# First gate weights split beside the input projection, half of layer 1's adaLN beside layer 0's attention, V projected amid head 0's K and Q

## The chip, the cores and the metric

The kernel runs on one core of one Trainium2 chip. The metric is the device time of one execution in microseconds, from 3 runs; a profile is one further execution. TensorE (PE; PEld is its weight load) multiplies matrices, VectorE (DVE) and ScalarE (ACT) work element by element and can read PSUM, GpSimd (POOL) works on SBUF, SyncE (SP) issues DMAs.

## The reference

Two layers of a diffusion backbone work on 1024 latent tokens and 256 context tokens of width 1024. Each layer modulates its input with adaLN, mixes tokens, gates the result with a SiLU branch, projects it, and normalises the sum with the residual:

```python
shift, scale, gate = adaln(c, ada_w[i], ada_b[i])        # silu(c) @ w + b, split in 3
shift_c, scale_c, gate_c = adaln(c_ctx, ada_w[i], ada_b[i])
h = x * (1.0 + scale[:, None, :]) + shift[:, None, :]
h_c = ctx * (1.0 + scale_c) + shift_c
...                                                      # token mixer i, gated
x = layer_norm(DEEPNORM_ALPHA * x + gate[:, None, :] * (o @ out_w[i]), ln_g[i], ln_b[i])
if need_ctx:
    ctx = layer_norm(DEEPNORM_ALPHA * ctx + gate_c * (o_c @ out_w[i]), ln_g[i], ln_b[i])
```

Layer 0 is multi-head latent attention with 16 heads: one projection of h gives a 256-wide Q latent, a 128-wide KV latent, 32 rotary key columns and the 1024 gate columns; the latents are RMS-normalised and projected up to Q, K (64 + 32 wide) and V (64 wide). Latent tokens attend to latent and context tokens, context tokens to the context. Layer 1 is differential attention with 8 heads.

## The kernel before, in words

Products of float32 operands are made of three matmuls (`mm3`, lines 185 to 188): each operand is split into a high part on ScalarE and a low remainder on VectorE or GpSimd (`split`, lines 176 to 178). Code that is not inside a `manual_schedule` block is reordered on each engine by a scheduler with a cost model, which takes the program order as preference; inside such a block the engines named (`MAN = 'P'`: TensorE alone) keep the written order. Pools of SBUF buffers are stacked from two sides; a tile waits until those that held its place have been read.

*Start (lines 204 to 238).* The shift and scale of layer 0 come from 16 loads of adaLN weights. Then h is made in three chunks, the context (256 tokens) and two of 512 latent tokens, in 8 parts each: load, high part on ScalarE, value on VectorE, remainder on VectorE, or on GpSimd for every third part.

*Input projection (lines 266 to 300).* Ten tiles of 128 tokens (context first), each 24 matmuls of 416 columns into PSUM tag "a" or "b" (two banks each). Squares on ScalarE, an inverse root on GpSimd (`rstd_of`) and a scaling on VectorE give the normalised rows `ln`; `lat_post` of the tile before follows: transposes through "c", split into `latH`, `latL`.

*Gates (lines 426 to 448).* The 1024 gate columns go in four quarters. For each, 8 rows of blocks of w_in are loaded and split (`wgs`, `wgH`, `wgL`), then 10 token tiles follow of 24 matmuls each, Silu on ScalarE, and a store to `sg_d` issued by SyncE. After each tile two steps of a generator `beside_gates` run. It holds, first, `up_weights` (lines 302 to 380): the split of the up-projections, the column norms of three weights (squares on ScalarE, a matmul with ones, a maximum on VectorE), the rotated key columns `kr`, and the power-of-two scales `vsc0`, `ksc0`, `qsc0`. Second, `ada_dve` (lines 383 to 419): layer 0's gate rows and all of layer 1's adaLN. Eight chunks (layer, pc) of 512 columns; each loads 8 blocks `adw` of 128 x 512 and adds them, times a column of silu(c), into `acc0` (latent) and `acc1` (context; not for the last two chunks) on VectorE. Matmuls with ones sum over the partitions. At the end `cols1` and `ab1` are made.

*Head 0 (lines 451 to 515, 708 to 715).* A new pool takes the place of h. V's weights are loaded and split in buffers "p32", which lie early in the pool. `prod_k` makes K of two heads at a time, `prod_q` Q with its rotary part; both store rows in a staging tile and copy them by DMA (`dmv`) to where the head needs them. `max0` computes row maxima of the scores on VectorE. `prod_v0` makes V, ten tiles, each in one pair of PSUM banks ("a", three pairs), evacuated by ScalarE and VectorE. In program order K and the first Q come first, then V's tiles with the rest of Q and the maxima between them.

*Attention (lines 605 to 735).* Each head has 11 units: 3 matmuls per 512 scores and key block, exponential and a float16 copy on ScalarE, a remainder on GpSimd (line 609), and the products with V two units later. Beside them run the next head's K, Q and maxima, as counts per unit (`run_step`), TensorE in written order. Head 15 also loads and splits the output weights (`load_outw`, lines 696 to 702).

After that come layer 0's output projection (lines 745 to 818) and layer 1 (from line 821), which the change does not touch.

## Time and profile before

| | us |
|---|---|
| median of 3 runs | 1950.05 |
| lowest, highest | 1944.06, 1951.67 |
| profiled execution | 1947.66 |
| its span, first to last instruction | 1945.9 |
| PE, DVE, ACT, POOL busy | 1749.7, 1283.0, 1033.5, 893.8 |
| mean granted clock of TensorE | 0.962 |

The rows quoted below are of this one execution; times in them count from the start of its span. A row of the timeline gives start, duration, engine, line, operation, output <- inputs, and in brackets the idle time before it with what ended it. A row of a group gives count, busy time, mean in ns, and the idle time before. A row of a window gives its length, the busy time and instructions of each engine (PE, PEld, DVE, ACT, POOL), the granted clock, the busy share of the DMA engines and GB/s.

### The profile page before, as it was taken

Reading aid. Unit: us, or ns where it says so; the run is one execution under the profiler, and the core shown is the slowest. Engines: PE = TensorE matmul, PEld = TensorE weight load, DVE = VectorE, ACT = ScalarE, POOL = GpSimd, SP = SyncE. Lnnn points to the kernel's source line nnn. Section 1 sums busy time; section 2 is a strip of 40 time slices with the busy share of each in tenths; the row PEclk is TensorE's granted clock in tenths of the full one; section 3 lists DMA queues with packets and bytes.
Section 4 is the critical chain, followed back from the end, with each engine's and each line's share of the span. In section 5 each row is a group of like instructions: output and inputs, shape, how many; then the busy total and the mean of one; then the engine's idle time right before and its main releaser. Section 6 shows DMA issues by size and latency. Waiting matters only on the chain. (4 is left out here: it accounts for less than half of the span.)

```text
span 1945.9 us, 36855 instructions
## 1 busy us (share of the span) xinstructions
PE 1749.7 (90%) x14460; PEld 1342.0 (69%) x14460; DVE 1283.0 (66%) x2213; ACT 1033.5 (53%) x2094; POOL 893.8 (46%) x750
## 2 busy tenths in 40 slices
PE   8889969999999998878879998989999999995997
PEld 2778945666666664556658787868787878783666
DVE  2536766666565658337753869686878787878785
ACT  2532127777777777701114565656666666665331
POOL 2433015767767676746663425242424242416322
PEclk9989979999999999989989999999999999997999
DMA  7426650111111113053233111111112121205331
GB/s 252 126 83 195 195 158 22 44 30 36 40 42 33 33 43 105 15 195 116 101 111 90 53 47 50 49 50 46 52 44 57 34 64 37 58 18 194 105 110 62
DMA packets 116366, 155.41 MB, mean 80 GB/s; under 512 B 14448, under 2 KB 85712, under 8 KB 116192
## 3 DMA queue, kind: packets, MB, share of 16 engines
q1 hardware_dynamic: 116192, 153.05, 25.8%
q8 instruction: 114, 1.87, 0.4%
q14 instruction: 60, 0.49, 0.1%
HBM read 99.18 MB, written 27.08 MB: 65 GB/s over the span
## 5 line engine op out<-in xcount | busy, mean ns | idle before, releaser
L609 POOL TENSOR_TENSOR pl<-p,ph 128x1024 f16<-128x1024 f32 (+1 forms) x176 | 362.7, 2066 | 185.7 <-ACT ph L608 160.7
L1046 ACT ACTIVATE p<-ps_b,mx 128x512 f32<-128x512 f32 (+1 forms) x384 | 232.8, 626 | 47.1 <-DVE mx L1043 46.6
L589 DVE TENSOR_REDUCE mx<-ps_a 128x1 f32<-128x1024 f32 x128 | 155.6, 1222 | 135.4 <-PE ps_a L587 135.4
L607 ACT ACTIVATE p<-ps_a,esc 128x1024 f32<-128x1024 f32 (+1 forms) x176 | 189.1, 1074 | 95.1 <-PE ps_a L665 88.4
L183 DVE SCALAR_TENSOR_TENSOR pl<-ps_b,lcf,ph 128x512 f16<-128x512 f32 (+1 forms) x192 | 123.3, 657 | 109.9 <-ACT ph L182 108.4
L608 ACT CAST ph<-p 128x1024 f16<-128x1024 f32 (+1 forms) x176 | 177.0, 1006 | 5.4
L1040 DVE TENSOR_REDUCE mx<-ps_b 128x1 f32<-128x512 f32 x256 | 166.0, 678 | 0.7 <-PE ps_b L1024 0.2
L186 PE MATMUL ps_b<-h1H,wH 128*128 128x512 f32 (+1 forms) x384 | 149.6, 390 | 18.7 <-ACT p L1046 15.7
L186 PE MATMUL ps_b<-wH,h1H 128*128 128x256 f32 x512 | 156.0, 305 | 0.0
L678 PE MATMUL ps_d<-Vh,pl 128*128 128x65 f16 x1344 | 147.6, 195 | 6.3 <-POOL pl L609 6.3
L675 PE MATMUL ps_d<-Vh,ph 128*128 128x65 f16 x1344 | 149.6, 196 | 0.0
L677 PE MATMUL ps_d<-Vl,ph 128*128 128x64 f16 x1344 | 148.3, 194 | 0.0
L187 PE MATMUL ps_b<-wL,h1H 128*128 128x256 f32 x512 | 146.7, 286 | 0.0
L188 PE MATMUL ps_b<-wH,h1L 128*128 128x256 f32 x512 | 146.5, 286 | 0.0
L182 ACT ACTIVATE ph<-ps_b,lcf 128x512 f16<-128x512 f32 (+1 forms) x192 | 120.5, 641 | 42.3 <-PE ps_b L1059 42.3
L188 PE MATMUL ps_b<-h1H,wL 128*128 128x512 f32 (+1 forms) x384 | 138.3, 360 | 4.2 <-POOL wL L178 4.2
L178 POOL TENSOR_TENSOR wL<-ws,wH 128x512 fp32r<-128x512 f32 x64 | 90.9, 1422 | 106.3 <-PE ps_b L187 59.0
L187 PE MATMUL ps_b<-h1L,wH 128*128 128x512 f32 (+1 forms) x384 | 137.7, 359 | 0.0
L675 PEld LDWEIGHTS <-ph 128*128 128x128 f16 x1344 | 124.2, 98 | 18.0 <-issue 5.0
L677 PEld LDWEIGHTS <-ph 128*128 128x128 f16 x1344 | 125.0, 99 | 12.4 <-issue 0.8
L1023 PE MATMUL ps_b<-KS,QS 128*128 128x512 f16 (+1 forms) x384 | 129.7, 355 | 3.8 <-ACT p L1046 2.7
L1024 PE MATMUL ps_b<-KS,Q 128*128 128x512 f16 (+1 forms) x384 | 132.3, 353 | 0.0
(338 smaller groups left out, 5389.4 us busy)
## 6 DMA issues: line engine op xcount, KB each, us to landing
adw<-in_ada_w SPq DMA_DIRECT2D x64, 256.0 KB
ws<-in_dw SPq DMA_DIRECT2D x64, 256.0 KB
g<-sg_d SPq DMA_DIRECT2D x18, 512.0 KB
adaw<-in_ada_w SPq DMA_DIRECT2D x16, 512.0 KB
sg_d<-gg SPq DMA_DIRECT2D x40, 128.0 KB
o<-o_d SPq DMA_DIRECT2D x10, 512.0 KB
o_d<-op SPq DMA_DIRECT2D x7, 640.0 KB
xt<-in_xT SPq DMA_DIRECT2D x16, 256.0 KB
```

The costliest lines, as they stand in the source:

```text
L186: pe.matmul(ps, aH, bH, start=start, stop=False, skip_group_check=skip)
L187: pe.matmul(ps, aH, bL, start=False, stop=False, skip_group_check=skip)
L188: pe.matmul(ps, aL, bH, start=False, stop=stop, skip_group_check=skip)
L589: dve.tensor_reduce(mx[:, t, 0:1], ps, axis=AX.X, op=ALU.max)
L607: act.activation(p32[:, :n], st, AF.Exp, scale=esc0)
L608: act.copy(ph[:, :n], p32[:, :n])
L609: pool.tensor_tensor(pl[:, :n], p32[:, :n], ph[:, :n], op=ALU.subtract)
L675: pe.matmul(pv[:, t, :], ph[:, ts], Vh[:, k, h, :], start=(k == kcs[0] and t == 0), stop=False, skip_group_check=True)
L677: pe.matmul(pv[:, t, :V0], ph[:, ts], Vl[:, k, h, :], start=False, stop=False, skip_group_check=True)
L678: pe.matmul(pv[:, t, :], pl[:, ts], Vh[:, k, h, :], start=False, stop=(k == NT - 1), skip_group_check=True)
L1040: dve.tensor_reduce(mx[:, 2 + 2 * m + i:3 + 2 * m + i], b, axis=AX.X, op=ALU.max, negate=True)
L1046: act.activation(p[m][:, c0:c0 + n], b, AF.Exp, bias=nb, scale=sc1, accum_out=sm[:, 2 + 3 * m + i:3 + 3 * m + i])
```

## The change

TensorE's written order (`man`) now holds from the input projection to the end of V.

1. The splitting of one part of h becomes `h_part`. The context and the first 512 latent tokens are split as before; the last 512 two parts at a time after each of the first four tiles of the projection, with three load buffers.
2. The first quarter's gate weights are loaded and split in the projection's loop, one block per tile; two of the quarter's tiles stand among the last two `lat_post`. The weights of a quarter are split during the quarter before, in two sets of buffers in two pools. The stores of the gates are issued by ScalarE.
3. `lat_post` follows its tile by two instead of one, and the normalisation has high priority.
4. In `up_weights` the rotated keys come ahead of the column norms, a norm's matmuls come a step after its squares, and V's weight for the norm is loaded by ScalarE.
5. `ada_dve` takes its buffers, banks and chunks as arguments; a chunk is closed at the eighth step of the next one. Four chunks remain beside the gates, (0, 4), (0, 5), (1, 0), (1, 1); (1, 2), (1, 3), (1, 4), (1, 5) run as a side of the attention, three steps per head, with two `adw` buffers and sums in the PSUM pairs. `ab1` is made after the attention.
6. "p32" moves to the end of the pool; V's weights use a third "p32" buffer for staging. `prod_v0` steps a whole tile, and starts after head 0's Q projection.

```diff
-    for i, (c0, n) in enumerate((CHUNKS[2], CHUNKS[0], CHUNKS[1])):
+    def h_part(pool_, bufs, c0, n, k):
         s = 0 if c0 < SEQ else 1
...
+    for i in (2, 0):
         for k in range(KT):
+            h_part(hs, 8, *CHUNKS[i], k)
...
+    pgr = p0.enter_context(spool("p0gr", side="right"))
+    def gate_w(pool_, q):
+        wH = pool_.tile([P, KT, 256], F32R, tag="wgH", bufs=1, name=nm("wgH"))
+        wL = pool_.tile([P, KT, 256], F32R, tag="wgL", bufs=1, name=nm("wgL"))
+        yield wH, wL
+        for k in range(KT):
+            ws = pgr.tile([P, 256], F32, tag="wgs", bufs=4, name=nm("wgs"))
+            sp.dma_start(ws, w_in[k * P:(k + 1) * P, NA + q * 256:NA + (q + 1) * 256])
+            split(wH[:, k, :], wL[:, k, :], ws, e_lo=pool)
+            yield
+    gcount = [0, 0, 0, 0]
+    def gate_tile(q, wH, wL):
+        t = gcount[q]
+        gcount[q] += 1
+        ts = slice(t * P, (t + 1) * P)
+        ps = bank("a" if t % 2 == 0 else "d")[:, :256]
+        for k in range(KT):
+            mm3(ps, hH[:, k, ts], hL[:, k, ts], wH[:, k, :], wL[:, k, :], k == 0, k == KT - 1)
+        g = pgr.tile([P, 256], F32, tag="gg", bufs=2, name=nm("gg"))
+        act.activation(g, ps, AF.Silu)
+        act.dma_start(sg_d[0][ts, q * 256:(q + 1) * 256], g)
+    gw = gate_w(pgr, 0)
+    wg = next(gw)
+    man = ExitStack()
+    man.enter_context(tc.manual_schedule(engines={ENG[c] for c in MAN}))
...
+        hk = iter(range(KT))
+        todo = []
+        for t in (8, 9, 0, 1, 2, 3, 4, 5, 6, 7, None, None):
+            if len(todo) == 2 or t is None:
+                lat_post(*todo.pop(0))
+                next(gw, None)
+            if t is None:
+                for _ in gw:
+                    pass
+                gate_tile(0, *wg)
+                continue
...
+            with tc.high_priority():
...
+            todo.append((t, ln))
+            for k in (next(hk, None), next(hk, None)):
+                if k is not None:
+                    h_part(pa, 3, *CHUNKS[1], k)
...
+                for j, f in enumerate(parts):
+                    f(wsq[:, j, :], slice(c0, c0 + 512))
+                yield
+                bk = bank("c")
+                for j, f in enumerate(parts):
+                    pe.matmul(bk, onr, wsq[:, j, :], start=j == 0, stop=j == len(parts) - 1)
...
+            act.dma_start(wv, w_kv[:, 1024 + c.start:1024 + c.stop])
...
+    def ada_dve(tile_, bk_, chunks):
+        def close(layer, pc, acc):
+            if pc < 4:
+                cb = bk_()
+                ns = len(acc)
+                for s in range(ns):
+                    for j in range(4):
+                        pe.matmul(cb[:, 2 * j + s:2 * j + s + 1], acc[s][:, j * P:(j + 1) * P], ones[:, 0:1],
+                                  start=True, stop=True)
...
+        for layer, pc in chunks:
+            acc = [tile_(f"acc{s}") for s in range(1 if layer and pc > 3 else 2)]
             for k in range(KT):
+                w = tile_("adw")
                 sp.dma_start(w, ada_w[layer, k * P:(k + 1) * P, pc * 512:(pc + 1) * 512])
...
+                if k == 7 and done:
+                    close(*done)
                 yield
+            done = layer, pc, acc
+        for _ in range(4):
             yield
+        close(*done)
+        yield
...
+            yield from ada_dve(t_, lambda: bank("c"), ((0, 4), (0, 5), (1, 0), (1, 1)))
...
+            for _ in gw:
+                pass
+            wH, wL = wg
+            if q < 3:
+                gw = gate_w((pg, pgr)[q % 2], q + 1)
+                wg = next(gw)
+            while gcount[q] < NT:
+                gate_tile(q, wH, wL)
+                if gcount[q] > 1:
+                    next(gw, None)
+                for _ in range(2 if q == 1 or q > 1 and gcount[q] % 5 < 3 else 1):
                     next(side, None)
...
+            "ows": ([P, D], F32, 2), "adw": ([P, 512], F32, 2), "acc0": ([P, 512], F32, 1),
+            "acc1": ([P, 512], F32, 1)}
...
     KL[0] = wk.tile([100, NTOK], F16, name="KL0")
+    TAG0["p32"] = [P, 1024], F32, PB[0]
+    rot(wk, *TAG0["p32"][:2], "p32", PB[0], first=True)
...
-    for _ in chain(prod_k(0), prod_q(0, 0)):
-        pass
-    vg, sg = prod_v0(), chain(max0(0, 0), prod_q(0, 1), prod_q(0, 2))
-    for i, _ in enumerate(vg):
-        if i % 2:
-            next(sg, None)
-    for _ in sg:
-        pass
+    vg = prod_v0()
+    if True:
+        for i, _ in enumerate(chain(prod_k(0), prod_q(0, 0), prod_q(0, 1), prod_q(0, 2), max0(0, 0))):
+            if i > 3:
+                next(vg, None)
+        for _ in vg:
+            pass
+    man.close()
+    ada = ada_dve(w0, pair, ((1, 2), (1, 3), (1, 4), (1, 5)))
...
+            run_step(units0(h, 0), [(ada, (0, 0, 1)), (max0(h, 1), (1, 1, 2, 1, 1)), (max0(h, 2), (0, 1, 0, 1)),
                                     (kq, (2, 2, 1 + quad, 0, 0) if even else (2,))])
...
+            run_step(units0(h, 1) + units0(h, 2), [(ada, (0, 0, 1, 0, 1)), (max0(h + 1, 0), (1, 1, 1, 2, 1)),
                                                    (qs, (1, 1 + quad, 0, 1) if even else (2,))])
     flush()
+    assert next(ada, 7) == 7
+    ab1_of()
```

163 lines of the change are left out of this document (63 added, 100 removed).

## The prediction

> **What bounds the kernel now.** I read the page first: TensorE is busy for most of the span, so time can be had where it stands idle.
>
> ```profile
> span 1945.9 us, 36855 instructions
> ...
> PE 1749.7 (90%) x14460; PEld 1342.0 (69%) x14460; DVE 1283.0 (66%) x2213; ACT 1033.5 (53%) x2094; POOL 893.8 (46%) x750
> ...
> PE   8889969999999998878879998989999999995997
> ```
>
> The low digits of the first 300 us are where the change works. I cut that stretch by stage with the windows view: span of the window, then busy time and instructions of PE, PEld, DVE, ACT, POOL, the granted clock, DMA.
>
> ```profile
> 42.25:62.20 19.95, 19.45 (x96) 17.42 (x96) 19.77 (x38) 15.75 (x26) 6.43 (x5) 1.00 0.72 229
> 62.20:67.04 4.84, 0.15 (x1) 0.00 (x0) 4.84 (x10) 1.66 (x8) 3.19 (x5) 0.75 0.21 65
> 67.04:107.50 40.46, 35.51 (x184) 32.42 (x184) 16.89 (x40) 18.30 (x66) 18.48 (x23) 0.92 0.21 61
> 107.50:119.20 11.70, 8.25 (x18) 4.72 (x19) 7.24 (x17) 6.79 (x14) 2.48 (x5) 0.50 0.22 59
> 119.20:252.05 132.85, 128.73 (x1028) 124.18 (x1027) 80.73 (x139) 25.98 (x68) 31.02 (x32) 0.99 0.60 180
> 252.05:264.30 12.25, 2.97 (x6) 0.17 (x5) 6.52 (x10) 0.38 (x1) 1.66 (x2) 0.65 0.57 172
> 264.30:304.90 40.60, 30.12 (x120) 20.62 (x119) 29.56 (x30) 15.75 (x18) 3.99 (x4) 0.85 0.36 105
> 312.00:745.00 433.00, 412.86 (x4917) 265.26 (x4917) 265.44 (x358) 332.42 (x331) 306.70 (x150) 1.00 0.14 36
> ```
>
> These are, in order: the input projection up to its fourth tile; a stop; the other six tiles; the column norms before the gates; the gate projection; the wait for layer 1's adaLN; head 0's K, Q and V up to the first score; and, past a short start, heads 0 to 14 of the attention. In the second row VectorE is full (4.84 of 4.84) while TensorE has one instruction; in the fourth the clock is 0.50 and TensorE does 18 instructions; in the sixth it does 6. In the last row TensorE is busy 95% with VectorE at 61%: there TensorE is the limit. The timeline of TensorE names what ended the stops (start, duration, idle before):
>
> ```profile
> 67.04 0.90 PE L271 MATMUL ps_c<-idr,ln 128*128 128x128 f32 x3 [4.69 <-DVE ln L293]
> ...
> 262.50 1.86 PE L405 MATMUL ps_b<-acc,ones 128*1 128x512 f32 x2 [9.18 <-DVE acc L396]
> 264.30 0.80 PE L186 MATMUL ps_a<-latH,wkH 128*128 128x512 f32 x1
> ...
> 282.69 1.03 PE L587 MATMUL ps_a<-KH,qH 96*128 96x512 f16 x2 [7.51 <-DMA qH<-stpH]
> ```
>
> So the front loses time to late VectorE work: normalised rows behind the splitting of h, the adaLN sums behind the loads of their own weights, and head 0's Q behind rope and a copy.
>
> **The change part by part.** *Input projection.* The lag between a tile's projection and its transposes grows from one tile to two, the normalisation gets priority over the splitting of h, the last 512 tokens of h are split between tiles, and TensorE keeps the written order. The price of a tile when nothing waits is the distance from one set of transposes to the next:
>
> ```profile
> 75.00 0.49 PE L271 MATMUL ps_c<-idr,ln 128*128 128x128 f32 x3
> ...
> 75.35 0.43 PE L186 MATMUL ps_b<-wAH,hH 128*128 128x416 f32 x1
> ...
> 79.98 0.49 PE L271 MATMUL ps_c<-idr,ln 128*128 128x128 f32 x3
> ```
>
> 4.98 us, ten tiles 49.8; from 42.25 that is 92. I add 5: the first four tiles are paced by h (19.95 us without a transpose, where 4 x (79.98 - 75.35) is 18.5), and the last parts of h may be late. VectorE's share of h is this:
>
> ```profile
> L235 DVE TENSOR_SCALAR xt<-xt,cols 128x512 f32<-128x512 f32 (+1 forms) x24 | 15.3, 681 | 0.8 <-ACT hH L234 0.7
> L237 DVE TENSOR_TENSOR hL<-xt,hH 128x512 fp32r<-128x512 f32 (+1 forms) x18 | 10.1, 590 | 0.0
> ```
>
> 25.4 us, and at most 1.7 for each tile's normalisation and split put before it (the third row above, 16.89 for ten): 42 + 25 + 4 x 1.7 = 74, and the seventh tile, the first to read those parts, is reached at 42.25 + 6 x 4.98 + 1.5 = 74. It just fits. Loads and splits of the first gate weights (8 DMAs, 8 ScalarE copies, 8 GpSimd subtractions) lie beside these matmuls; their buffers lie where the staging of the start lay, which is free once token 511 of h is split. If they were late, the gates would wait as they do now. Queued on TensorE behind a late transpose are the next tile and all after it, which is why the lag matters; two tiles are 10 us of cover, and the stop now is 4.69. Gates start at 97 instead of 119.20 (the first few come before that, at half the rate): **-22** (-26 if nothing waits, -11 if half of it does).
>
> *Gate stage.* A gate matmul takes 0.12 us from start to start; the small adaLN matmuls are 16 records in 1.84, or two in 1.02:
>
> ```profile
> 237.67 0.28 PE L186 MATMUL ps_d<-wgH,hH 128*128 128x256 f32 x1
> 237.79 0.28 PE L187 MATMUL ps_d<-wgL,hH 128*128 128x256 f32 x1
> ...
> 241.63 1.84 PE L402 MATMUL ps_c<-ones,acc 128*128 128x1 f32 x16
> ...
> 252.30 1.02 PE L405 MATMUL ps_b<-acc,ones 128*1 128x512 f32 x2
> 267.38 0.40 PE L188 MATMUL ps_a<-latH,wqL 128*128 128x512 f32 x1
> 267.61 0.39 PE L186 MATMUL ps_a<-latH,wqH 128*128 128x512 f32 x1
> ...
> L326 PE MATMUL ps_c<-wsq,onr 128*128 128x512 f32 x9 | 6.6, 775 | 4.1 <-DVE vm L327 1.4 <-ACT wsq L337 0.9 <-ACT wsq L340 0.7
> ```
>
> The column norms move in here, square and matmul a gate tile apart. Their ten matmuls cost at most the 0.775 us each of the half clock, at least the 0.23 from 267.38 to 267.61; I take the low value, since the clock of the gate stage is 0.99: 2.4 us. 40 tiles of 24: 115.2. Layer 0's gates (four sums) 4.1, half of layer 1's columns 3.7, norms 2.4: 125.4, and 2 for waits, 127.4 against 132.85 now: **-5.5**. The forty stores leave SyncE's queue for ScalarE's, an engine that is busy 25.98 of 132.85; SyncE's loads no longer stand behind a Silu. VectorE's 64 steps and 32 loads remain beside 125 us of matmuls; the closing sums come at the eighth step of the next chunk, so TensorE finds them done.
>
> *The wait of 12.25* goes: prod_k follows the last gate tile. **-12.25.** What is late next is head 0.
>
> *Head 0.* V's weights lie at a place that is free before the last quarter of the gates, and V's tiles start after Q's projection, between the copies. Then VectorE limits. It starts 3.7 us after K's first matmul:
>
> ```profile
> 267.96 1.68 DVE L183 SCALAR_TENSOR_TENSOR stkL<-ps_a,ksc,stkH 128x1024 f16<-128x1024 f32 x2 [2.88 <-ACT stkH L182]
> ...
> L493 DVE SCALAR_TENSOR_TENSOR Vl<-ps_a,vsc,Vh 128x1024 f16<-128x1024 f32 x10 | 12.8, 1279 | 2.9 <-ACT Vh L492 2.9
> L262 DVE TENSOR_SCALAR rr<-rr,gkva 128x512 f32<-128x512 f32 x1 | 1.3, 1251 | 1.1 <-DMA rr<-in_w_kv 1.1
> ...
> L262 DVE TENSOR_SCALAR rsw<-rsw,gkva 128x512 f32<-128x512 f32 x1 | 0.5, 489 | 0.0
> ```
>
> Its 29.56 us of the window lose the V weights' scaling (1.25 and 0.49) and gain the tenth V tile that now comes later (1.28): 29.1. With 3.7 before and 1.5 of gaps 34.3 against 40.60: **-6.3** (-7.8 without gaps, 0 if the copies still end last).
>
> First score at 304.9 - 46 = 259.
>
> *Attention.* Four chunks move here: 32 loads on SyncE, 48 VectorE steps, the sums. On SyncE's queue the loads stand among the copies of K's and Q's rows, which a load that waits for its buffer holds up. Sums on TensorE: 3.7 + 2.0 = **+5.7**, moved, so counted in full. Steps:
>
> ```profile
> L396 DVE SCALAR_TENSOR_TENSOR acc<-adw,sc,acc 128x512 f32<-128x512 f32 x98 | 68.8, 751 | 20.2 <-DMA adw<-in_ada_w 20.0
> L589 DVE TENSOR_REDUCE mx<-ps_a 128x1 f32<-128x1024 f32 x108 | 131.2, 1222 | 120.2 <-PE ps_a L587 120.2
> ```
>
> 36 us in all. VectorE idles 120.2/108 = 1.1 us ahead of each row maximum, which covers one step of 0.75, not two. Behind a waiting step stand row maxima, and behind those TensorE, for want of one of three PSUM pairs. Below nothing it can't be: TensorE gets no work less here. The nearest row is head 15, where VectorE and ScalarE also split the output weights:
>
> ```profile
> 745.00:760.00 15.00, 12.35 (x169) 7.84 (x168) 14.63 (x12) 12.26 (x14) 10.36 (x5) 1.00 0.57 151
> 760.00:775.00 15.00, 10.16 (x113) 6.15 (x110) 13.20 (x15) 11.64 (x12) 8.46 (x4) 0.87 0.54 164
> ...
> L701 DVE SCALAR_TENSOR_TENSOR oL<-ows,usc,oH 128x1024 fp32r<-128x1024 f32 x8 | 16.5, 2068 | 1.9 <-ACT oH L700 1.8
> ```
>
> TensorE idles 7.5 us of 30, against 1.4 at the attention's 4.7%: 6.1 lost by eight steps of 16.5 us. By busy time that is 0.37 for each us, 13 for our 36; by count 0.76 each, 37 for 48. I take **+13**, since our steps are half as long; bounds 0 and 37.
>
> Here a rule speaks against the change. L701 is the same kind of step, with two operands in SBUF beside GpSimd's subtraction L609:
>
> ```profile
> L701 DVE SCALAR_TENSOR_TENSOR oL<-ows,usc,oH x8: 1268/1883/3187, 745.2 to 775.7; 128x1024 fp32r<-128x1024 f32 x8
> L609 POOL TENSOR_TENSOR pl<-p,ph x176: 1151/2129/3002, 311.0 to 820.7; 128x1024 f16<-128x1024 f32 x160, 128x512 f16<-128x512 f32 x16
> ```
>
> (Least, median, most, in ns.) It varies from 1.27 to 3.19 us. The Trainium skill, "SBUF — State Buffer", section "Who interferes with whom", says why that may be: a VectorE instruction with two SBUF inputs and a GpSimd one that reads SBUF exclude each other for a whole instruction. By that rule our steps, which in the gate stage had an idle GpSimd beside them, grow in the attention; the trace agrees as far as L701's spread goes.
>
> **Sum.** -22 - 5.5 - 12.25 - 6.3 + 5.7 + 13 = -27.4. The profiled execution took 1947.66 us (span and 1.76 around it): 1920.3. The median of the runs is 2.4 higher; the same gain there gives 1922.7. I say 1921.
>
> **Rivals.**
> 1. *The steps hide entirely.* For: the 1.1 us. Against: two steps in one turn are 1.5. 1947.66 - 46.05 + 5.7 = 1907.
> 2. *The fixed order waits in front* (the change doesn't do what it says): h is late for the seventh tile, gates start at 108, head 0 still ends with its copies. For: VectorE is full to 67. -11 - 5.5 - 12.25 + 18.7: 1937.6.
> 3. *VectorE and GpSimd exclude each other* and each step costs TensorE what one of L701 did, 0.76: +36.7, so 1944. Against: L701 also had a ScalarE copy of 1.14 us with it. This is the rule of the Trainium skill above, priced by rows.
> 4. *Slower: each step waits for its load.* Two buffers and VectorE's order could set each step behind a landing, with the row maxima behind it. The landing:
>
> ```profile
> L390 SPq DMA_DIRECT2D adw<-in_ada_w x64: 327/328/1315, 156.2 to 258.7; - x64
> L394 DVE TENSOR_SCALAR acc<-adw,sc x14: 468/486/948, 159.7 to 253.2; 128x512 f32<-128x512 f32 x14
> ```
>
> First issue 156.2, first step 159.7: 3.5 us, less the 1.1 of slack, times 32: +77, so 1984. It makes the kernel slower by over 0.5% from 1.64 us for each load on (52.5 over 32). Against: DMA is 0.14 busy in the attention, loads are issued a step or more ahead, and the mean wait now, at 0.60, is 20.0/98.
>
> **How the numbers follow.** Forecast 0.54, rival 1 0.17, rival 2 0.15, rival 3 0.10, rival 4 0.04. The range takes in rival 1 with the front's best end (-26 - 5.5 - 12.25 - 7.8 = -51.5: 1902) and the noise of the runs below it, and rival 3 above: 1900 to 1944. Some 0.5% is what a measurement of this kernel can tell from no change, here 1940.3 to 1959.8: faster 0.84 (forecast, 1, nearly all of 2), same 0.12 (rival 3 and the tail of 2), slower 0.04.
>
> **What would show it.** In the trace after: no stop of TensorE over 1 us between 48 and 95; first gate matmul near 97; last gate matmul near 224 and K's first right behind it; first score near 259; from there to the end of head 14 some 19 us more than the 440 now, with VectorE's row maxima waiting less. L396's median in the attention tells rival 3 (above 1.2), its waits for adw rival 4. Wrong would be: a later first gate, a new stop on V's weights or the column norms, or an attention longer by 40.

## The result and the profile after

The changed kernel takes **1959.7 us** (median of 19 runs, 1951.04 to 1962.19), the kernel before 1946.47 (19 runs, 1936.66 to 1952.1). The ratio is 1.0067, with a 95% interval of 1.0053 to 1.0081: slower, where 1921 was forecast and 1944 was the end of the range. The profiled execution took 1958.66, 11.0 more than that of before. The page's head:

```profile
span 1956.8 us, 36836 instructions
...
PE 1761.9 (90%) x14460; PEld 1355.2 (69%) x14460; DVE 1296.7 (66%) x2216; ACT 1033.9 (53%) x2094; POOL 893.1 (46%) x750
...
PE   8899988998989899869879999999999999995997
```

TensorE executes as many matmuls as before and is busy 12.2 us longer with them. Where, the windows view of the changed kernel tells (length, busy time and instructions of PE, PEld, DVE, ACT, POOL, granted clock, DMA share, GB/s). Its rows are the input projection up to its first transposes, the stretch behind them, the rest of the projection, the gates, the stretch up to K's first product, head 0's K, Q and V up to the first score, and the attention up to the last reciprocal:

```profile
42.95:58.53 15.58, 11.03 (x49) 9.89 (x49) 15.27 (x33) 11.10 (x23) 6.57 (x8) 0.83 0.71 221
58.53:63.08 4.55, 4.55 (x15) 4.32 (x16) 4.05 (x9) 4.15 (x11) 1.24 (x2) 0.50 0.06 23
63.08:103.20 40.12, 38.23 (x215) 36.98 (x214) 15.24 (x31) 16.57 (x60) 16.36 (x24) 1.00 0.20 61
103.20:238.30 135.10, 128.23 (x1003) 123.36 (x1000) 64.97 (x115) 36.03 (x89) 31.35 (x37) 0.96 0.49 140
238.30:246.21 7.91, 3.59 (x19) 3.44 (x17) 4.33 (x8) 0.38 (x1) 1.98 (x2) 0.67 0.88 287
246.21:285.26 39.05, 31.35 (x119) 22.07 (x120) 30.81 (x34) 16.99 (x18) 2.58 (x2) 0.89 0.32 87
285.26:836.16 550.90, 503.35 (x5818) 321.14 (x5817) 365.94 (x473) 398.15 (x395) 366.87 (x176) 0.97 0.19 52
```

The same stretch of the kernel before, from its first score to its last reciprocal:

```profile
304.90:824.32 519.42, 485.06 (x5782) 309.58 (x5781) 317.21 (x419) 399.01 (x396) 362.74 (x176) 0.99 0.15 40
```

| | before | forecast | after | change |
|---|---|---|---|---|
| first gate at full rate | 119.20 | 97 | 103.20 | -16.0 |
| last gate | 252.05 | 224 | 238.3 | stage +2.25 |
| K's first product | 264.30 | 224 | 246.21 | wait -4.3 |
| first score | 304.89 | 259 | 285.26 | stage -1.55 |
| last reciprocal | 824.32 | | 836.16 | stage +31.5 |
| end of the span | 1945.9 | | 1956.8 | rest -1.0 |

The front won 19.6 us in place of 46, and the attention lost 31.5 in place of 18.7. The 31.5 is half waiting and half slow work: TensorE's idle time there grew from 34.4 to 47.6 (13.2), its busy time by 18.3, of which the closing sums account for 3.5 (by two runs below); the rest goes with a clock of 0.97 instead of 0.99.

What ended TensorE's longest stops in the front, from its timeline in the changed kernel (start, duration, idle before with what ended it):

```profile
58.53 0.90 PE L305 MATMUL ps_c<-idr,ln 128*128 128x128 f32 x3 [4.55 <-DVE ln L337]
...
134.89 0.40 PE L186 MATMUL ps_a<-wgH,hH 128*128 128x256 f32 x1 [2.22 <-ACT gg L293]
...
150.09 0.80 PE L388 MATMUL ps_c<-wsq,onr 128*128 128x512 f32 x1 [4.60 <-ACT wsq L399]
...
242.77 3.57 PE L437 MATMUL ps_c<-ones,acc 128*128 128x1 f32 x16 [4.32 <-DVE acc L462]
```

A normalisation that VectorE ends, the Silu of a gate tile, a Square on ScalarE that a column norm is made from, and the last adaLN steps: each is work of another engine that stood at a fixed place in TensorE's written order and came late. The first of them was late on three engines. The matmuls of its tile had ended at 49.5, but its Square on ScalarE, its inverse root on GpSimd and its scaling on VectorE each stood behind that engine's share of h:

```profile
54.76 0.36 ACT L332 ACTIVATE junk<-ps_a 128x256 f32<-128x256 f32 x1
56.59 0.25 POOL L156 TENSOR_SCALAR rs<-ss 128x2 f32<-128x2 f32 x1
57.99 0.48 DVE L337 TENSOR_SCALAR ln<-ps_a,rs 128x256 f32<-128x256 f32 x1
```

In the attention the steps are not one or two to a unit. A chunk's sums have one buffer each and are closed at the eighth step of the next chunk, so none of the next chunk's 16 steps can start before; then they come at once. VectorE's timeline in the second of the four chunks, with a row maximum's reduction (L654) between:

```profile
475.51 3.05 DVE L462 SCALAR_TENSOR_TENSOR acc<-adw,sc,acc 128x512 f32<-128x512 f32 x4
478.49 0.15 DVE L654 TENSOR_REDUCE ng<-mx 128x4 fp32r<-128x8 f32 x1
...
480.79 2.81 DVE L462 SCALAR_TENSOR_TENSOR acc<-adw,sc,acc 128x512 f32<-128x512 f32 x4 [0.98 <-DMA adw<-in_ada_w]
483.51 1.22 DVE L648 TENSOR_REDUCE mx<-ps_a 128x1 f32<-128x1024 f32 x1
```

Reduction L654, which joins the row maxima, stands behind four steps; TensorE's waits between 464 and 488 show what that cost (total, times, longest):

```profile
PE ps_a L657 <- DVE ng L654: 2.8, 1, 2.8
PE ps_a L722 <- DVE cols L439: 2.2, 1, 2.2
```

Comparing the 48 reciprocals of both kernels pair by pair, counted from the first score, the distance grows only in four places: by 10.3 at the first, by 12.2 around 475, by 5.5 around 570 and by 9.4 around 660; everywhere else by at most 1.1, and head 15 gives 4.9 back. These are the four chunks. That was my first theory: **the packing** holds up the row maxima and is the loss.

### The profile page after: what moved, and what is told of

Read it like the earlier page. It is cut to its first block, busy times and chain, and to the rows that moved or that the text cites. A ratio compares the mean times of both kernels' runs of the same rounds, so it can differ in the third digit from the quotient of the medians.

```text
span 1956.8 us, 36836 instructions
## 1 busy us (share of the span) xinstructions
PE 1761.9 (90%) x14460; PEld 1355.2 (69%) x14460; DVE 1296.7 (66%) x2216; ACT 1033.9 (53%) x2094; POOL 893.1 (46%) x750
## 5 line engine op out<-in xcount | busy, mean ns | idle before, releaser
L668 POOL TENSOR_TENSOR pl<-p,ph 128x1024 f16<-128x1024 f32 (+1 forms) x176 | 366.9, 2091 | 210.8 <-ACT ph L667 198.7
L737 PE MATMUL ps_d<-Vh,pl 128*128 128x65 f16 x1344 | 153.4, 196 | 10.0 <-POOL pl L668 8.7
L734 PE MATMUL ps_d<-Vh,ph 128*128 128x65 f16 x1344 | 157.0, 197 | 0.0
L736 PE MATMUL ps_d<-Vl,ph 128*128 128x64 f16 x1344 | 155.4, 195 | 0.0
L722 PE MATMUL ps_a<-qH,KH 100*128 100x512 f16 x320 | 124.6, 390 | 12.0 <-ACT p L666 2.6
L737 PEld LDWEIGHTS <-pl 128*128 128x128 f16 x1344 | 125.5, 99 | 13.0 <-POOL pl L668 12.9
```

The costliest lines, as they stand in the source:

```text
L668: pool.tensor_tensor(pl[:, :n], p32[:, :n], ph[:, :n], op=ALU.subtract)
L734: pe.matmul(pv[:, t, :], ph[:, ts], Vh[:, k, h, :], start=(k == kcs[0] and t == 0), stop=False, skip_group_check=True)
L736: pe.matmul(pv[:, t, :V0], ph[:, ts], Vl[:, k, h, :], start=False, stop=False, skip_group_check=True)
L737: pe.matmul(pv[:, t, :], pl[:, ts], Vh[:, k, h, :], start=False, stop=(k == NT - 1), skip_group_check=True)
```

## The experiments

**Theory 1** was the packing. **Theory 2**: a step costs wherever it stands on VectorE. **Theory 3**: the loads on SyncE's queue cost. "Attention" is always the time from the first score to the last reciprocal, 519.4 before and 550.9 after. Nine kernels below have the changed kernel's front; with it, their first scores lie between 284.3 and 287.6, so a shift under some 3 us there tells nothing.

### What the steps in the attention cost

**Steps kept in place.** Each step is queued behind the last row maximum written before it; the sums get a second buffer.

```diff
-                for s, a_ in enumerate(acc):
+                with tc.issue_after(dl[0]) if dl[0] else nullcontext():
+                    for s, a_ in enumerate(acc):
...
+                dl[0] = dve.tensor_reduce(mx[:, t, 0:1], ps, axis=AX.X, op=ALU.max).ins
```

> Each adaLN step of the attention is kept on VectorE behind the row maximum written before it, and the two sums of a chunk lie in one of the two rows buffers that are idle until head 15, so that the next chunk's first product no longer waits for the sums to be closed. Number and work of the steps stay as in the changed kernel. Theory 1 (steps packed into four bursts that hold up the row maxima cost the attention its 31.5 us): from the first score to the last reciprocal 519.4 + 5.7 (closing sums) up to + 13, so 525 to 533 instead of 550.9, the first score stays near 285, time 1934 to 1942. Theory 2 (each step has its price wherever it stands, as VectorE busy time was 317 and is 366): the attention stays at 545 to 551, time 1954 to 1960. Theory 3 (the loads on SyncE's queue hold up the copies of Q and K): they are as many as before, the attention stays over 540, time over 1949.

Time 1960.35, ratio to before 1.0076 (1.0051 to 1.0101), attention 548.6. Theory 1's figure is missed by 16 us. The jumps are gone, and in their place nearly every step costs something: over eleven heads the distance to before grows on, by up to 5.9 us from one reciprocal to the next. The windows row of the attention and the steps' own durations (least, median, most in ns):

```profile
286.80:835.38 548.58, 497.69 (x5818) 318.62 (x5817) 394.36 (x476) 398.29 (x395) 365.72 (x176) 0.98 0.20 54
```

```profile
L465 DVE SCALAR_TENSOR_TENSOR ows<-adw,sc,ows x42: 736/2146/2714, 309.5 to 660.3; 128x512 f32<-128x512 f32 x42
```

VectorE is busy 28.4 us longer than in the changed kernel with the same number of steps. The median step takes 2146 ns; in the changed kernel's attention it was 752, in the gate stage of before 746.

**The same with one buffer for each sum**, and **the second buffer without keeping the steps in place**:

> The steps are kept behind the row maximum written before them, as in the run before, but the two sums keep their one buffer each, so that the second, third and fourth chunk's steps can still start only when the sums before are closed, at the written place of the last load. Theory 1: the first burst goes (10.3 us), the other three stay (12.2, 5.5 and 9.4): attention about 541 instead of 550.9, time about 1949. Theory 2: attention 545 to 551. Theory 3: over 545, as nothing is changed for the loads but their time.

> Only the sums get their second buffer (in the rows buffers idle until head 15), the steps stay free for the scheduler to place. In the order that it makes, the first two chunks' steps lie one behind the other in the first two heads, and the third and fourth each right behind a close. Theory 1: the bursts are not gone but thinner, the attention stays at 535 to 551; a buffer alone is not the cure. If the attention falls under 533, the missing buffer alone was the cause and not the freedom of the order. Theory 2: 545 to 551.

Attention 550.4 and 546.8 (times 1956.94 and 1955.37, one run each). With one buffer the first jump shrank from 10.3 to 3.7, but the first chunk's cost came back step by step, 13.6 in all against 9.7. With two buffers and a free order the first two chunks together cost 22. Whether packed or spread, the total hardly moves: Theory 1 falls as the explanation of the size.

**Loads without steps, steps without loads, products without sums.** Each of the three leaves out a part of the adaLN that the attention makes.

```diff
-                    else:
+                    elif not late:
                         dve.scalar_tensor_tensor(a_, w, ck, a_, op0=ALU.mult, op1=ALU.add)
```

> The 32 loads of adaLN in the attention stay as in the changed kernel, but of VectorE's steps there only the first of each chunk is made (the accumulating steps are left out: the half of layer 1's adaLN done in the attention is wrong by that). Theory 2 (VectorE's steps cost, wherever they stand): attention 519.4 + 5.7 for the closing sums + at most 3, so 525 to 529, time about 1934. Theory 3 (the loads, SyncE's queue and the DMA traffic cost): attention over 540.

```diff
-                w = tile_("adw")
-                sp.dma_start(w, ada_w[layer, k * P:(k + 1) * P, pc * 512:(pc + 1) * 512])
+                if k == 0 or not late:
+                    w = tile_("adw")
+                    sp.dma_start(w, ada_w[layer, k * P:(k + 1) * P, pc * 512:(pc + 1) * 512])
```

> The steps stay, the loads go: each chunk of the attention loads its first 128 rows only and makes all eight steps from them (rows 2 to 8 of a chunk are left out of the result). Theory 2: the attention stays at 541 to 551, as VectorE does the same work. Theory 3: under 533.

```diff
+                    elif late:
+                        dve.tensor_scalar_mul(a_, w, ck)
                     else:
```

> All loads, and in place of each accumulating step a product alone, with one input from SBUF and not two (the sums are left out, so the half of adaLN done in the attention is wrong). Alone, the product took 0.48 us in the changed kernel and the step 0.72; beside GpSimd's subtraction L668 the step took 1.77 to 1.89 on average. If the stretch beside GpSimd is the cost (two SBUF inputs), the products stay near 0.48 and the attention falls to 525 to 533. If each us of VectorE costs a us, 48 x 0.48 = 23 us of it stay, so 535 to 546. Theory 3: 545 to 551.

Attention 517.6, 553.6 and 545.9; times 1927.97, 1960.21 and 1953.68, one run each. The windows row of the first:

```profile
287.00:804.59 517.59, 488.84 (x5818) 314.80 (x5817) 320.76 (x432) 397.77 (x395) 363.74 (x176) 0.99 0.20 55
```

All 32 loads are there, the DMA share is 0.20, and the attention is no longer than before (it is shorter than expected, since head 15 became 4.9 us shorter, which no theory had). Without the loads nothing is won. Theory 3 falls, Theory 2 stands: 42 accumulating steps cost 550.9 - 517.6 = 33.3 us of attention for 365.9 - 320.8 = 45.1 us of VectorE, 0.74 for each. The products without sums cost 28.3 for 37.5, nearly the same (0.76), and here the stretch is easy to see:

```profile
L462 DVE TENSOR_SCALAR acc<-adw,sc x42: 470/486/2417, 285.5 to 665.7; 128x512 f32<-128x512 f32 x42
```

Sorted by what GpSimd did at the time (both timelines laid over each other), the 21 products that met no subtraction of GpSimd took 0.48 us on average, the 17 with one beside them for more than half of their time 1.73. My expectation that one input from SBUF would not be stretched was wrong. The Trainium skill, "SBUF — State Buffer", section "Who interferes with whom", lists a product with a scalar among the VectorE operations that can run in a mode which takes the port pair shared with GpSimd, so that one of the two waits for a whole instruction; the trace agrees in the durations, and no run here shows the port itself.

**Off VectorE.** ScalarE makes the products, GpSimd adds.

```diff
+                            act.activation(m_, w, AF.Copy, scale=sc[:, 2 * k + s:2 * k + s + 1])
+                            if k:
+                                pool.tensor_tensor(a_, a_, m_, op=ALU.add)
```

> Off VectorE: in the attention ScalarE makes the products and GpSimd adds them up, each kept behind the cast and the subtraction of its unit; the two sums lie in one of the rows buffers idle until head 15, the weights have four buffers. Nothing of the computation is left out. Theory 2 (VectorE is what the steps cost): attention 525 to 531, first score near 286, time 1934 to 1940, faster than both kernels. If GpSimd's additions (about 1 us each, 42 of them, by L668's 2.09 us for twice the elements) only move the wait to the value product's wait for pl, attention 540 or more and time 1950 or more.

Time 1950.32, ratio 1.0016 (1.0000 to 1.0031), attention 541.7: the second of the two outcomes. Here the pairwise distances told more than the sum. The 16 loads with one sum cost some 3 us together; the 16 with two cost some 17, with TensorE's value product waiting for GpSimd (10.5 us up to 440); and at 565 there is a single jump of 7.2. VectorE's timeline there, and TensorE's wait:

```profile
560.04 2.06 DVE L485 TENSOR_TENSOR ab<-lng,cols 128x8 f32<-128x8 f32 x1
...
564.48 0.74 DVE L667 SCALAR_TENSOR_TENSOR qH<-ps_a,sh,selt 4x512 f16<-4x512 f32 x1
```

```profile
PE ps_a L731 <- DVE qH L667: 3.9, 1, 3.9
```

This is `ab1_of`, written behind the attention. Its inputs are ready when the chunk (1, 3) is closed, so the scheduler sets it there, ahead of a query row; operations on 8 columns take up to 2.06 us. So the next run makes **one addition to a place and keeps `ab1_of` last**:

```diff
+                        if s < len(acc) - 1:
+                            yield
...
-            run_step(units0(h, 0), [(ada, (0, 0, 1)), (max0(h, 1), ...
+            run_step(units0(h, 0), [(ada, (0, 0, 1, 0, 1)), (max0(h, 1), ...
...
+    with tc.issue_after(dl[2]):
+        ab1_of()
```

> As the run with ScalarE's products and GpSimd's additions, but one addition to a place in place of two (four places per head in place of three), and ab1 (five small VectorE operations) kept behind the attention's last output on VectorE. In the run before, the 16 loads with one sum cost 3 us together and the 16 with two sums some 17; ab1 stood ahead of a query row that TensorE waited 3.9 us for. If it is what is queued behind them that makes the price, one at a time costs 0.2 us each: attention 518 (as with loads alone) + 8 = 524 to 530, time 1932 to 1938, faster than both kernels. If each addition has its price wherever it stands (0.35 us by the run before), 534 or more and time 1942 or more.

Time **1935.16**, ratio 0.9947 (0.9930 to 0.9964), attention 524.7: as expected, and faster than both kernels. Where `ab1_of` had made the jump of 7.2 the distance now grows by 1.3; the rest of the 17.0 us is the additions. 48 steps cost 524.7 - 517.6 = 7.1 us of the attention:

```profile
284.30:809.02 524.72, 487.84 (x5818) 315.45 (x5817) 316.10 (x420) 426.32 (x443) 416.80 (x218) 1.00 0.21 56
```

GpSimd's busy time rose by 53 us against the run of loads alone, ScalarE's by 29, and TensorE's clock is 1.00. To tell whether place or engine did this, **the same places with VectorE**:

> VectorE makes the steps again, one to a place (four places per head), each kept behind the row maximum written before it; two sums' buffers, ab1 behind the attention's last output, as in the run with one addition to a place on GpSimd (attention 524.7). This is the spread that the prediction's 13 us assumed. If only the packing of the steps cost, the waits of VectorE hide most of each: attention 525 to 531. If a step costs on VectorE wherever it stands (beside GpSimd's subtraction it took 1.77 us and not 0.72, and the 16 single steps of the first run's last two chunks cost some 0.5 us each): 517.6 with loads alone + 48 x 0.5 = 538 to 546.

Attention 543.5, time 1952.96. One at a time, in the places where GpSimd's additions cost 7.1, VectorE's steps cost 25.9. The rows of VectorE's steps and of TensorE's longest wait in the attention:

```profile
L465 DVE SCALAR_TENSOR_TENSOR ows<-adw,sc,ows x42: 743/1679/2699, 309.0 to 699.7; 128x512 f32<-128x512 f32 x42
```

```profile
PE ps_a L726 <- DVE qH L662: 19.5, 27, 1.5
```

VectorE's busy time is 391.2, 70.4 over the loads alone: 0.37 of attention for each us, half of the packed price, but for over one and a half times the us, since a step behind a row maximum falls beside GpSimd's subtraction. 40 of the 42 steps had it beside them for more than half of their time and took 1.66 us on average; of the packed steps of the changed kernel 14 had, at 2.00 us, and 23 met no subtraction, at 0.75. The run with the steps kept in place, two to a place, lies between: 31.0 us of attention for 73.6 of VectorE, 0.42 each. So packed steps are short and hold up more, spread steps hold up less and are long. (This run has two buffers for the loads where the one with GpSimd has four, but VectorE never sat idle for a load in its attention.)

### The front

**All eight chunks beside the gates.**

```diff
-            yield from ada_dve(t_, lambda: bank("c"), ((0, 4), (0, 5), (1, 0), (1, 1)))
+            yield from ada_dve(t_, lambda: bank("c"), ((0, 4), (0, 5), (1, 0), (1, 1), (1, 2), (1, 3), (1, 4), (1, 5)))
...
-                for _ in range(2 if q == 1 or q > 1 and gcount[q] % 5 < 3 else 1):
+                for _ in range((1, 2, 3, 3)[q]):
```

> All eight chunks of adaLN beside the gates again, none in the attention; all else as in the changed kernel. Theory 1 and 2 alike: the attention is back at 519 to 522. The front pays: the changed kernel still waited 4.3 us for its half of the steps and then closed them in 3.6; with the whole, 32 loads more between 150 and the end of the gates, the wait should be that of before (12.3) or more, so the first score near 293 to 300, time 1934 to 1943. If the first score stays near 285, the half moved into the attention bought nothing and time is near 1928.

Time 1968.06, ratio 1.0115 (1.0087 to 1.0143). The attention is below that of before, but the last gate comes at 276.3 and the first score at 331.5, 31 us past what I expected. TensorE's wait for the sums of the gate rows and the attention's row:

```profile
PE ps_c L445 <- DVE acc L462: 18.9, 3, 8.8
```

```profile
331.50:845.36 513.86, 485.38 (x5782) 311.78 (x5781) 313.09 (x416) 397.91 (x395) 363.24 (x176) 0.99 0.15 40
```

TensorE's fixed order now waits for adaLN inside the gates too: this front, as its loop is paced, has no room for the whole of adaLN. The row of the attention also prices the closing sums there, against the run with loads alone: 517.6 - 513.9 = 3.7 us, 3.5 of them TensorE's busy time.

The next runs stand on the run with one addition to a place (first score 284.3). **Three tiles of lag**:

```diff
-        for t in (8, 9, 0, 1, 2, 3, 4, 5, 6, 7, None, None):
-            if len(todo) == 2 or t is None:
+        for t in (8, 9, 0, 1, 2, 3, 4, 5, 6, 7, None, None, None):
+            if len(todo) == 3 or t is None:
```

> The run with one addition to a place, and the transposes of a latent tile written three tiles behind its projection in place of two. If VectorE's late first normalisation is what TensorE stops for at 58.5 (4.55 us, then 18.5 us at clock 0.87), stop and low clock go and the first gate comes at 97 to 99 in place of 103.2, the first score 4 to 6 us before 285. If VectorE has too much to do up to there, the stop only comes one tile later: first gate over 101.

The first gate comes at 97.1, the forecast's figure, and the stop is gone. The windows rows of this run, split at the same place as above:

```profile
42.95:58.50 15.55, 15.32 (x65) 14.47 (x66) 15.24 (x32) 11.29 (x24) 6.35 (x7) 0.79 0.72 222
58.50:97.10 38.60, 37.19 (x209) 35.70 (x208) 19.12 (x39) 19.13 (x68) 16.85 (x25) 1.00 0.22 65
```

TensorE is busy 15.3 of the first 15.6 us, where it was 11.0. But of the 6.1 us only 2.9 reach the first score (281.4; time 1930.63): TensorE then waits 8.5 us for the Square and 8.9 for the last adaLN steps.

**The norm's value weights loaded ahead, the gate weights' low halves on VectorE**:

```diff
+        wvn = [pa.tile([P, 512], F32, tag="wvn", name=nm("wvn"))]
+        act.dma_start(wvn[0], w_kv[:, 1024:1536])
...
-            split(wH[:, k, :], wL[:, k, :], ws, e_lo=pool)
+            split(wH[:, k, :], wL[:, k, :], ws, e_lo=pool if q == 0 else dve)
```

> The run with one addition to a place; the value weights for the norm are loaded ahead (the first half at the start of the up-projection weights, the second right behind the first Square), and VectorE in place of GpSimd makes the low halves of the gate weights from the second quarter on. If ScalarE's queue (a Square that waits for its load) and GpSimd's backlog (buffers of the gate weights freed late, so loads and casts late) make the two stops between 130 and 151 (2.5 and 4.9 us) and the low clock after them, both go: gates 127 to 130 us in place of 135.1, first score 276 to 281. If the stops come from elsewhere, the gates stay at 133 to 136.

First score 277.3, time 1927.01, but not for the reason given: the gate stage stayed at 134.8 us, as long as without this edit, and the wait for the Square grew from 3.5 to 6.6. What was won is the wait for adaLN behind the gates (2.1 us from the last gate to K's first product, in place of 9.4). Which of the two edits won it wasn't told apart.

**A fifth chunk moved into the attention**, alone, then with both repairs; and **both repairs without it**:

> The run with one addition to a place; three of eight chunks beside the gates and five in the attention, five places per head. If the loads of the last steps beside the gates are what the closing waits for (4.3 us, then 3.6 at half clock, and the value weights' loads behind them), the first score comes 5 to 10 us earlier than 285, and the attention pays 16 additions, 3 to 8 us. If the gates end is bound elsewhere, the first score stays and the time rises by 3 to 8 against the run with four chunks.

> The run with one addition to a place, with both repairs of the front: transposes three tiles behind, and the value weights loaded ahead with VectorE making the gate weights' low halves. Alone they brought the first score to 281.4 and 277.3, from 284.3. If the front's losses lie in a row, they add up: first gate at 97, first score 271 to 275, time 1919 to 1925. If the closing of adaLN beside the gates is the floor (its loads ended at 239), K's first product stays at 237 to 240 whatever the gates do, first score 275 to 278, time 1925 to 1929.

> The run before with three chunks beside the gates and five in the attention. If adaLN's loads are the floor at the gates' end, taking a chunk from them brings the first score to 264 to 271; the attention pays about 9 us, as it did when this was done alone (533.9 against 524.7): time within 3 us of the run before. If the floor is elsewhere, the first score stays within 2 us and the time rises by 7 to 11.

Alone, the fifth chunk brought K's first product right behind the last gate (247.85), but that gate came 9.9 later; the first score stayed at 283.4, the attention paid 9.2 and the time was 1934.85. Both repairs without it: **1923.64**, ratio **0.9884 (0.9867 to 0.9901)**, first gate at 95.4, first score 276.7: the floor of the second forecast. With it: K's first product at 232.2, right behind the last gate, first score 267.7, but attention 538.1, time 1928.55, ratio 0.9899 (0.9878 to 0.9920). TensorE's timeline in the run without it (the profiled execution took 1929.19) shows what remains:

```profile
142.55 0.80 PE L390 MATMUL ps_c<-wsq,onr 128*128 128x512 f32 x1 [8.80 <-ACT wsq L399]
...
235.11 3.54 PE L442 MATMUL ps_c<-ones,acc 128*128 128x1 f32 x16 [4.92 <-DVE acc L477]
238.51 0.77 PE L186 MATMUL ps_a<-latH,wkH 128*128 128x512 f32 x1
```

The Square is late because of what ScalarE takes ahead of it: the four casts of the query weights, which share one staging buffer with their load and GpSimd's subtraction, and then eight casts of the next quarter's gate weights, the last four of which wait for their loads. In the changed kernel's timeline of ScalarE:

```profile
117.23 0.84 ACT L177 CAST wqH<-ws 128x768 fp32r<-128x768 f32 x1 [4.01 <-DMA sg_d<-gg]
124.47 0.83 ACT L177 CAST wqH<-ws 128x768 fp32r<-128x768 f32 x1 [2.42 <-DVE ws L353]
...
140.42 0.84 ACT L177 CAST wqH<-ws 128x768 fp32r<-128x768 f32 x1 [4.75 <-DVE ws L353]
...
145.99 0.40 ACT L177 CAST wgH<-wgs 128x256 fp32r<-128x256 f32 x1 [1.90 <-DMA wgs<-in_w_in]
...
149.33 0.71 ACT L399 ACTIVATE wsq<-wkv,gkva 128x512 fp32r<-128x512 f32 x1
```

Two runs ask whether the one buffer is to blame or a written place that is too early: **a second staging buffer** (without the value weights loaded ahead), and **the norms six places later**.

```diff
-                ws = pa.tile([P, 768], F32, tag="ws2", bufs=1, name=nm("ws2"))
+                ws = pa.tile([P, 768], F32, tag="ws2", bufs=2, name=nm("ws2"))
```

> The run with both repairs of the front, but in place of the value weights loaded ahead, the staging of the query up-projection weights gets a second buffer. In the changed kernel the four casts of these weights start at 117.2, 124.5, 133.7 and 140.4, one load and one GpSimd subtraction apart, and stand ahead of the second Square on ScalarE; with the repairs TensorE still stopped 8.8 us for that Square (133.5 to 142.5). If the one buffer is what paces them, the stop shrinks below 3 us, the gate stage to 122 to 126 us (from 129.9) and adaLN beside the gates starts and ends earlier: first score 268 to 273, time 1915 to 1921. If SyncE's order of loads paces them, the stop stays over 5 and the first score at 275 to 279.

```diff
+        for _ in range(6):
+            yield
         vm = pa.tile([P, 8], F32, name="vm")
```

> The run with both repairs of the front and the column norms six places later in the loop beside the gates (the last two quarters then give one place more in five). If it is only TensorE's written order that meets a late Square, the stop of 8.8 goes, but adaLN's steps start six places later and its loads end as late as before: first score 274 to 279, time within 4 us of that run (1923.6). If the stop only moves along, the first score comes over 280.

The gate stage that the first of these texts gives as 129.9 us ends with the last tile but one; the whole stage took 134.7. The second buffer halved the stop, 8.8 to 4.4, and the stage took 130.7; the first score, 275.4, is the one named for the other cause. So the one buffer is at most a part of it. The later place removed the stop, and the stage took 126.4, with the first score at 272.6, earlier than forecast. The times are 1924.13, ratio 0.9898 (0.9875 to 0.9921), and **1922.97**, ratio 0.9890 (0.9865 to 0.9914): no different from the run with both repairs. The windows rows of the gates and of what follows them, with the norms later:

```profile
95.40:221.85 126.45, 124.16 (x992) 119.64 (x990) 71.38 (x132) 36.56 (x91) 14.23 (x13) 0.99 0.49 141
221.85:237.00 15.15, 5.28 (x35) 5.20 (x33) 9.79 (x15) 0.38 (x1) 1.99 (x2) 0.58 0.76 231
```

The gates end at 221.8, before the 224 of the forecast, and K starts at 237.0 all the same. In the three runs with the longer lag, VectorE's low halves and four chunks beside the gates, the gates end at 230.0, 228.3 and 221.8, and K starts at 238.5, 237.2 and 237.0. That is a floor, and it is the half of adaLN beside the gates: in the run of 1923.64 us its 32 loads are issued from 170.5 to 230.2, and with one chunk fewer K started right behind the gates. In that stretch SyncE waited 25 us for VectorE's steps to free one of the three `adw` buffers, and VectorE 18 us for loads to land; more buffers were not tried, so what paces the floor stays open.

**The order of V**, put back on the run with one addition to a place:

```diff
-        for i, _ in enumerate(chain(prod_k(0), prod_q(0, 0), prod_q(0, 1), prod_q(0, 2), max0(0, 0))):
-            if i > 3:
-                next(vg, None)
+        for _ in chain(prod_k(0), prod_q(0, 0)):
+            pass
+        sg = chain(max0(0, 0), prod_q(0, 1), prod_q(0, 2))
+        for _ in vg:
+            next(sg, None)
```

> The run with one addition to a place, with V's projection in the order of the kernel before (K and the first Q wholly ahead of it, the first row maxima and the other Q inside it), all else as there (first score 284.3, head 0's stage 36.9). If the changed order is worth what the prediction took, the first score comes 4 to 7 us later, at 288 to 291; if VectorE's work bounds the stage in both orders, within 2 us.

First score 285.5 in place of 284.3, time 1936.69: inside the scatter. From K's first product to the first score it takes 38.8 us and not 36.9. The order of V is worth 2 us at most here.

## Why the prediction was wrong, point by point

1. **Input projection, -22: it was -16.0.** The step that failed is "two tiles are 10 us of cover", which counted VectorE's work alone. The Square, the inverse root and the scaling of the first normalisation all stood behind h on their engines, and VectorE made the last of them only when it had split all eight parts of the first latent chunk (58.0), priority or not; TensorE stopped 4.55 us and then ran at clock 0.50 to 63.1. With three tiles of cover the first gate comes at 97.1: the price of a tile and the start were right.
2. **Gate stage, -5.5: it was +2.25.** The content was right (126.4 us once the Square no longer stops it, against 125.4 worked out). "And 2 for waits" failed: the norms' matmuls stand one gate tile behind their Squares in TensorE's order, and the Squares stand in ScalarE's queue behind casts that wait for a staging buffer or a load. I counted ScalarE's busy share there (26 us of 133) and not what its queue waits for.
3. **The wait of 12.25 goes: it shrank to 7.9.** "TensorE finds them done" holds for every chunk but the last. Its steps end when its last load has landed, and the closing then takes 3.6 us at clock 0.50. In the runs with four chunks beside the gates and the first gate at 95 to 98, K still starts at 237 or later, not at 224.
4. **Head 0, -6.3: it was -1.55.** VectorE was busy 30.8 us, not 29.1, and TensorE ran at clock 0.89. The order by itself is worth at most 2 us; how the rest of the stage divides was not settled.
5. **Attention, +18.7: it was +31.5**, namely 33.3 for the steps, 3.7 for the closing sums (5.7 forecast) and -5.5 that comes without any adaLN there. The step that failed is "I take +13". The rule was that 36 us of VectorE cost 0.37 each. The price was 0.74, where the steps came packed: one buffer for each sum and a close seven steps late forbid the spread that the counts per unit describe, and that can be read in the code. And the us were 45 and not 36, because of GpSimd. With the spread made true the price is 0.37, but the us are 70. That the figure comes out so exactly is in part luck: it was read from head 15, where ScalarE's casts run too, and the same eight steps there take 14.0 us in the changed kernel and not 16.5, in a head that is 4.9 us shorter. The bound by count, 37, was nearer than the value taken. Rival 3 gave the steps 36.7 and they cost 33.3: its mechanism, VectorE and GpSimd in each other's way, is a part of it. In the changed kernel packing doubled the price (0.74 for 0.37) and the stretch added two fifths to the time (45 us for 42 steps that take 31 alone); in the spread run the price was the forecast's and the stretch more than doubled the time (70 for 31). The sign that I named for it, a median over 1.2 us, failed in the changed kernel: its median was 752 ns, since over half of the packed steps (23 of 42) met no subtraction; their mean was 1178.
6. **Rival 1** (the steps hide entirely) is out by the 33.3 us. **Rival 4** (each step waits for its load) is out: the attention with all loads and no sums is as long as before. **Rival 2** had the front's mechanism right, TensorE's fixed order waiting for others, at other places than it named.

Sum as measured: -16.0 + 2.25 - 4.3 - 1.55 + 31.5 - 1.0 = +10.9, and the profiled executions differ by 11.0. The forecast's front and attention errors are 26.4 and 12.8 us; the first alone would have left it 1 us faster by the sum, which is inside the scatter. Not settled: head 15 is 4.9 us shorter in the changed kernel and in the runs made from it, also in the one that has no adaLN in its attention.

## What to carry to other kernels

Work put on an engine that is 61% busy isn't free if that engine's results are the next thing in the written order of the engine that limits: read what waits behind it, give it to an engine whose result is needed later, one small piece to a place, and check in the code that buffers and closings permit the spread that the counts describe. Where one engine keeps a written order, each place in it is a due time for all the others; look for what stands ahead in their queues, not at how busy they are. And price a move by the stage that it leaves as well: whatever stays there may be the floor.

## What the runs showed of the hardware

A stop of TensorE can be paid about twice. In the run with the steps kept in place, TensorE's timeline shows two stops within three us, and then the same matmul at two durations; the windows row is the stretch with the low clock:

```profile
408.50 0.38 PE L724 MATMUL ps_a<-qH,KH 100*128 100x512 f16 x1 [2.15 <-DVE mx L650]
...
410.83 1.01 PE L654 MATMUL ps_a<-KH,qH 96*128 96x256 f16 x4 [0.86 <-DVE mx L650]
...
413.10 0.62 PE L724 MATMUL ps_a<-qH,KH 100*128 100x512 f16 x1
...
416.90 0.38 PE L724 MATMUL ps_a<-qH,KH 100*128 100x512 f16 x1
```

```profile
409.83:416.66 6.83, 5.97 (x54) 3.74 (x52) 4.59 (x6) 2.88 (x3) 2.12 (x1) 0.50 0.10 26
```

From 413.1 to 415.8 the score matmuls take 0.62 to 0.63 us, before and after 0.38. The two stops together were 3.0 us; the 5.97 us of work at a clock of 0.50 cost, as an estimate, as much again. Over the whole attention, 14.5 of the 33.3 us that the steps cost (by TensorE's busy time against the run of loads alone) are longer busy time and no waiting.

Who pays when VectorE and GpSimd meet depends on the stage. In the attention a VectorE step of 0.75 us alone took 1.66 to 2.00 on average beside GpSimd's subtraction, while that subtraction hardly changes (median 2131 ns with the steps, 2128 without): there the price falls on VectorE. In the gate stage of the kernel before, where 12 of the 98 steps met a subtraction and six steps come in a row, it fell on GpSimd. The steps kept their length, and a subtraction whose median is 740 ns took 4.60 us:

```profile
186.52 4.04 DVE L396 SCALAR_TENSOR_TENSOR acc<-adw,sc,acc 128x512 f32<-128x512 f32 x6
186.57 4.60 POOL L178 TENSOR_TENSOR wgL<-wgs,wgH 128x256 fp32r<-128x256 f32 x1
```

No run here varied which of the two started first.
